# A decoder layer in one kernel: transposed FFN operands stored in parts, x1 loaded a step ahead, the mixer's output sums moved

## Chip, cores and metric

One core of a Trainium2 chip runs the whole kernel. The metric is device time in microseconds, from the first instruction to the last. The kernel before has a median of 1925.28 us over 3 runs (1925.04 to 1928.67).

## What is computed

One decoder layer over 2048 rows of 1024 columns in float32, with a gated-MLP mixer and a SwiGLU feed-forward (2816 hidden), each modulated by six vectors made from `c`:

```python
mod = silu(c) @ mod_w + mod_b
sh1, sc1, g1, sh2, sc2, g2 = split(mod, 6)
h = x * (1 + sc1) + sh1
u, v = split(gelu(h @ w_in + b_in), 2)
v = layer_norm(v, ln_g, ln_b)                    # 1024 columns
sv = w_m @ v per chunk of 128 rows and group of 128 columns + b_s   # w_m: w_s * causal
y = (u * sv) @ w_out
x = layer_norm(ALPHA * x + (1 + g1) * y)         # x1
h = x * (1 + sc2) + sh2                          # h2
g, u = split(h @ ffn_w_in, 2)
y = (silu(g) * u) @ ffn_w_out
out = layer_norm(ALPHA * x + (1 + g2) * y)
```

## The kernel before

**Products in parts.** Every large product runs on TensorE with both operands split into two parts: `parts` (lines 91 to 96) makes hi as a cast on ScalarE (line 94) and lo as a subtraction on VectorE (line 95), both into one tile of 4 KB per partition (UNIT). Three matmuls per product follow, hi by hi, hi by lo, lo by hi. The mixer's output weights `wot` are prepared early and kept in DRAM already in parts; they are loaded straight into the tiles that TensorE reads.

**Rows.** The rows stand in four blocks b of 512, and in two halves sb of two blocks. The mixer (line 274) runs for one half, then for the other: the v product with its layer norm, eight u steps (`u_tile`; a step is two blocks by 24 matmuls) with the spatial products (`s_tile`) from step 3 on, then y.

**y.** y is a Strassen-Winograd product: seven smaller products P1, P2, P6, P5, P7, P3, P4 in that order, each over four k. Their left operands are blocks of u and sums of them: `left_y` (line 388) makes the four sums per k on VectorE (line 393) when P6's operands are made, and then the parts (tiles `y_S`, tag hB). P6, P7 and P4 accumulate in the banks in which P1 lies, after `evacuate` has taken P1's values out (line 409: x times a constant plus the bank, into row r), with x loaded into an xs buffer. Two layer-norm passes follow per half, and x1 goes to DRAM (`x1d`).

**The FFN's left operands.** `h2_part` (line 459) takes one pair of 128-column slices of x1 for one block: TensorE transposes it (line 475), ScalarE modulates (line 476). The FFN is a Strassen-Winograd product too, over blocks A11, A12 (from the even block) and A21, A22 (odd block) with sums S1 to S4. So for the even block A11 and A12 go raw to DRAM (`hop`), and for the odd block they are read back, GpSimd forms the sums (four of them), and A22 and S1 to S4 go raw to `hop`. `tail` (line 782) is the load of x1 (`x1c`, four DMAs) and `h2_part`. The first half's eight tails run in the u steps 0 to 3 of the second half's mixer, two in a step; the second half's run inside the FFN loop. `load_ops` (line 503) reads `hop` and makes the parts, just before the FFN uses them: 28 tiles per half.

**The FFN.** `ffn_in` (line 517) takes 11 column groups, each with seven products for gate and up; the weights' parts are made four products ahead. `ffn_out` (line 669) is the last product.

**What sets the order.** Nearly all DMAs go through SP's one queue in program order, so a DMA that waits holds those behind it. A framework's scheduler fixes each engine's order ahead of time, from the code's order, its own costs and the pools' buffers: lt and xs have 3 row buffers each, late 10, hB 8, w 6, u 16 half rows; in the FFN h3 has 4 rows and hr 2 half rows. A new tile in a buffer waits until the old one's last reader is through, and a DMA store counts as a reader.

Of the kernel before, what the change touches and what calls it, by code (L numbers as in the profile page):

```python
# [37 lines left out]
def gmlp_swiglu_layer(  # L38
# [235 lines left out]
    def mixer(sb, jobs, u_done):  # L274
# [8 lines left out]
        def h_piece(d):  # L283
            if sc1[d] is None:
                mod_of(sh1, 0, d, 0.0, "lt")()
                mod_of(sc1, 1, d, 1.0, ("lc", "bc")[d % 2])()
            for x, b in enumerate(blocks):
                r = new("u", f"xT{b}_{d}", HALF)
                nc.sync.dma_start(out=r, in_=xT[d, :, b * TB : (b + 1) * TB])
                nc.scalar.activation(r, r, AF.Identity, bias=sh1[d], scale=sc1[d])  # L290
                h[x][d] = parts(r, f"h{b}_{d}", ("hA", "hB")[x])
# [211 lines left out]
    def load_ops(sb, names):  # L503
# [277 lines left out]

    def tail(b, i, tag):
# [4 lines left out]
        h2_part(b, i, lambda t, q: x1[:, t, q, :], tag)  # L787

# [99 lines left out]
```

## Time and profile before

| | |
|---|---|
| median of 3 runs | 1925.28 us |
| the profiled execution's own time | 1928.73 us |
| its span in the profile | 1927.0 us |
| TensorE matmuls, weight loads | 1840.4 us (96%), 1519.8 us (79%) |
| VectorE, ScalarE, GpSimd | 1228.4, 688.6, 505.4 us |
| mean granted TensorE clock | 0.979 of full |
| DMA | 359.69 MB, mean 187 GB/s |

TensorE's busy share is an average over stages that differ; the idle time lies in a few places, and after a stop the clock is at its lower level for a while. So the places are read one at a time: the list of waits, then a table of stretches, and in each stretch the chain or the timeline. A matmul of 512 columns shows more than its step in such a list, since successive ones overlap.

### The profile page before, as it was taken

What the parts mean: (1) busy time and instruction counts of PE and PEld (TensorE: products, weight loads), DVE (VectorE), ACT (ScalarE), POOL (GpSimd) and SP (SyncE); (2) the same over time, 40 slices, a digit from 0 to 9 for tenths busy, and PEclk for the clock granted to TensorE, in tenths of its full rate; (3) what the DMA queues carried; (4) which work ended last, traced back from release to release, by engine and by line L of the source; (5) the groups of instructions that cost most, each with busy time, mean ns of one, the idle gap of its engine ahead of it and who ended that gap; (6) DMA issues with size and microseconds to landing.
All of it is one profiled execution on the core that took longest, in us unless ns stands there. A gap on an engine that the chain in (4) does not pass through costs nothing.

```text
span 1927.0 us, 23234 instructions
## 1 busy us (share of the span) xinstructions
PE 1840.4 (96%) x8168; PEld 1519.8 (79%) x8168; DVE 1228.4 (64%) x1785; ACT 688.6 (36%) x1132; POOL 505.4 (26%) x327
## 2 busy tenths in 40 slices
PE   7999989997978799999999999999999999999997
PEld 6888877875867588888887888888888888888886
DVE  7569878241676965545777856767766344446868
ACT  5264152152221443443334533333334233334320
POOL 0000000003000456556543455355533100000104
PEclk9999999998989899999999999999999999999998
DMA  9638875136565634554455535654554666556532
GB/s 379 200 133 318 316 271 197 65 110 207 181 239 193 221 117 170 190 170 149 167 196 179 174 104 192 206 170 159 193 196 170 223 191 187 180 174 185 169 128 98
DMA packets 171015, 359.69 MB, mean 187 GB/s; under 512 B 19953, under 2 KB 36369, under 8 KB 170898
## 3 DMA queue, kind: packets, MB, share of 16 engines
q1 hardware_dynamic: 170834, 358.17, 55.0%
q8 instruction: 64, 1.05, 0.2%
q14 instruction: 53, 0.43, 0.1%
q0 software_dynamic: 64, 0.03, 0.0%
HBM read 251.43 MB, written 106.70 MB: 186 GB/s over the span
## 4 chain that ended last, share of the span: by engine, by line
PE 80%; issue 8%; DVE 5%; DMA 4%; ACT 1%; POOL 1%; SPq 0%; DVEq 0%; POOLq 0%; ACTq 0%
PE o L663 21%; PE v_ps L312 8%; PE u_ps L346 6%; PE y L448 1%; PE f_10g_X L521 1%; PE f_4g_X L521 1%; PE f_2g_X L521 1%; PE f_3g_X L521 1%; PE f_5g_X L521 1%; PE f_1u_X L521 1%; PE f_4u_X L521 1%; PE f_3u_X L521 1%; PE f_2u_X L521 1%; PE f_5u_X L521 1%; PE f_1g_X L521 1%
## 5 line engine op out<-in xcount | busy, mean ns | idle before, releaser
L663 PE MATMUL o<-wd_w,alw 128*128 128x512 f32 x1848 | 419.2, 389 | 0.0
L663 PEld LDWEIGHTS o<-wd_w,alw 128*128 128x128 f32 x1848 | 346.8, 188 | 72.0
L183 POOL TENSOR_TENSOR ln_rss<-ln_ves,mhalf 128x4 f32<-128x4 f32 x7 | 14.4, 2050 | 708.5 <-DVE ln_ves L182 708.5
L312 PE MATMUL v_ps<-wv,h 128*128 128x512 f32 x768 | 178.4, 395 | 16.3 <-ACT h L94 12.5
L346 PE MATMUL u_ps<-h,wu 128*128 128x512 f32 x768 | 185.8, 401 | 2.8 <-ACT wu L94 2.8
L312 PEld LDWEIGHTS v_ps<-wv,h 128*128 128x128 f32 x768 | 146.4, 191 | 47.8 <-ACT h L94 13.0
L448 PE MATMUL y<-y_T,y_S 128*128 128x512 f32 x672 | 161.1, 401 | 18.2 <-ACT y_S L94 12.5
L346 PEld LDWEIGHTS u_ps<-h,wu 128*128 128x128 f32 x768 | 147.0, 193 | 33.9 <-ACT wu L94 3.2
L448 PEld LDWEIGHTS y<-y_T,y_S 128*128 128x128 f32 x672 | 129.8, 194 | 48.7 <-ACT y_S L94 14.5
L95 DVE TENSOR_TENSOR alw<-al,alw 128x512 fp32r<-128x512 f32 x154 | 100.3, 686 | 88.3 <-ACT alw L94 88.3
L94 ACT CAST alw<-al 128x512 fp32r<-128x512 f32 x154 | 89.0, 620 | 142.1 <-PE o L663 139.9
L95 DVE TENSOR_TENSOR wd_w<-wdl,wd_w 128x512 fp32r<-128x512 f32 x77 | 52.9, 689 | 67.1 <-ACT wd_w L94 67.1
L94 ACT CAST wd_w<-wdl 128x512 fp32r<-128x512 f32 x77 | 47.8, 623 | 105.0 <-PE o L663 79.8
L119 DVE SCALAR_TENSOR_TENSOR modw<-modw,cact 128x1024 f32<-128x1024 f32 x48 | 58.4, 1219 | 25.0 <-DMA modw<-in_modwT 25.0
L95 DVE TENSOR_TENSOR wu<-wu_raw,wu 128x512 fp32r<-128x512 f32 x32 | 22.2, 701 | 67.0 <-ACT wu L94 67.0
L351 ACT ACTIVATE u<-u_ps,colc 128x512 f32<-128x512 f32 x32 | 22.0, 689 | 88.1 <-PE u_ps L346 88.1
L94 ACT CAST y_S<-u 128x512 fp32r<-128x512 f32 x48 | 29.2, 620 | 59.3 <-PE y L448 25.7
L95 DVE TENSOR_TENSOR y_S<-u,y_S 128x512 fp32r<-128x512 f32 x48 | 32.4, 685 | 21.5 <-ACT y_S L94 21.5
L94 ACT CAST wv<-wv_raw 128x512 fp32r<-128x512 f32 x32 | 19.8, 620 | 73.2 <-PE v_ps L312 44.9
L183 POOL TENSOR_TENSOR lnv_rss<-lnv_ves,mhalf 128x4 f32<-128x4 f32 x4 | 4.8, 1206 | 156.4 <-ACT wu L94 90.3
L617 DVE TENSOR_TENSOR wd<-wd,g_bc 128x512 f32<-128x512 f32 x44 | 36.5, 855 | 14.0 <-DMA wd<-in_wd 13.6
L95 DVE TENSOR_TENSOR wv<-wv_raw,wv 128x512 fp32r<-128x512 f32 x32 | 21.8, 683 | 25.9 <-ACT wv L94 25.9
(615 smaller groups left out, 3702.9 us busy)
## 6 DMA issues: line engine op xcount, KB each, us to landing
al<-aop SPq DMA_DIRECT2D x154, 256.0 KB, 2.9
modw<-in_modwT SPq DMA_DIRECT2D x48, 512.0 KB, 6.2
aop<-aop_s SPq DMA_DIRECT2D x88, 256.0 KB, 2.0
y_T<-woT SPq DMA_DIRECT2D x32, 512.0 KB, 4.9
y_T<-woB SPq DMA_DIRECT2D x24, 512.0 KB, 6.1
wd<-in_wd SPq DMA_DIRECT2D x44, 256.0 KB, 4.2
wdT<-wd SPq DMA_DIRECT2D x44, 256.0 KB, 4.4
wdl<-wdT SPq DMA_DIRECT2D x44, 256.0 KB, 2.7
```

What stands on the lines that cost most here:

```text
L94: nc.scalar.copy(out=o[:, 0, :], in_=src)
L95: nc.vector.tensor_tensor(out=o[:, 1, :], in0=src, in1=o[:, 0, :].bitcast(F32), op=ALU.subtract)
L119: nc.vector.scalar_tensor_tensor(out=w, in0=w, scalar=1.0, in1=env["cact"], op0=ALU.mult, op1=ALU.mult, accum_out=modc[:, j : j + 1],)
L183: nc.gpsimd.tensor_tensor(out=rs, in0=ve, in1=mhalf.broadcast_to([P, m]), op=ALU.pow)
L312: nc.tensor.matmul(ps[x][t], lhsT=h[x][k][:, part, t * P : (t + 1) * P], rhs=w[:, wpart, :], start=(k == 0 and part == 0 and wpart == 0), ...
L346: nc.tensor.matmul(p, lhsT=w[d // 4][:, wpart, (d % 4) * P : (d % 4 + 1) * P], rhs=h[x][d][:, part, :], start=(d == 0 and wpart == 0 and p ...
L351: nc.scalar.activation(u[x, i], p, AF.Gelu, bias=colc[:, i : i + 1])
L448: nc.tensor.matmul(ps[j], lhsT=a[:, part, j * P : (j + 1) * P], rhs=w[:, wpart, :], start=(k == 0 and part == 0 and wpart == 0 and pr in ( ...
L521: nc.tensor.matmul(ps, lhsT=w[:, wpart, k * P : (k + 1) * P], rhs=a[k][:, part, :], start=(first and k == 0 and wpart == 0 and part == 0), ...
L617: nc.vector.tensor_tensor(out=b, in0=b, in1=env["g2"][:, cs], op=ALU.mult)
L663: nc.tensor.matmul(ps[:, cs], lhsT=a[:, part, p * P : (p + 1) * P], rhs=w[:, wpart, cs], start=(first and part == 0 and wpart == 0), stop= ...
```

## The change

Four things are done.

1. **Parts in DRAM.** `hop` tiles hold parts (512 KB instead of 256). `store` makes the parts where the operand is made, in buffers that alternate between two tags (xs and lt for the first half, h3 and hr for the second), and stores them; `load_ops` loads 28 tiles of parts per half and makes nothing. Since the odd block needs raw A11 and A12, these go raw to new DRAM tiles `hraw` as well. hr is now one full tile.
2. **x1 a step ahead.** `tail_load` is split from `tail`; the first load is issued in the v product, and each step issues the next one's, into a late buffer. There is one tail per u step, 0 to 7, instead of two in each of steps 0 to 3. The columns of g2 (eight modw loads) move from u steps 4 to 7 to steps 6 and 7.
3. **xT of the second half** lies in lt buffers instead of u buffers.
4. **y's sums** are made after the parts of P1 (two of them) and of P2 (the other two).

```diff
-    hop = [[[dram.tile([P, TB], F32, name=f"hop{o}_{k}_{sb}") for sb in range(2)] for k in range(NK)] for o in range(7)]
+    hop = [[[dram.tile([P, 2, TB], F32, name=f"hop{o}_{k}_{sb}") for sb in range(2)] for k in range(NK)] for o in range(7)]
+    hraw = [[[dram.tile([P, TB], F32, name=f"hraw{q}_{k}_{sb}") for sb in range(2)] for k in range(NK)] for q in range(2)]
...
-                r = new("u", f"xT{b}_{d}", HALF)
+                r = new("lt" if sb else "u", f"xT{b}_{d}", HALF)
...
-            if pr == 6:
-                for o, a, b, op in ((t, a21, a22, ALU.add), (a21, a11, a21, ALU.subtract), (a11, t, a11, ALU.subtract), (a12, a12, a11, ALU.subtract)):
-                    nc.vector.tensor_tensor(out=o, in0=a, in1=b, op=op)
-            return parts({1: a11, 2: a12, 6: a11, 5: t, 7: a21, 3: a12, 4: a22}[pr], f"y{sb}_S{pr}{k}", "hB")
+            p = parts({1: a11, 2: a12, 6: a11, 5: t, 7: a21, 3: a12, 4: a22}[pr], f"y{sb}_S{pr}{k}", "hB")
+            sums = {
+                1: ((t, a21, a22, ALU.add), (a21, a11, a21, ALU.subtract)),
+                2: ((a11, t, a11, ALU.subtract), (a12, a12, a11, ALU.subtract)),
+            }
+            for o, a, b, op in sums.get(pr, ()):
+                nc.vector.tensor_tensor(out=o, in0=a, in1=b, op=op)
+            return p
...
         def store(n, src):
-            nc.sync.dma_start(out=hop[A_AT[n]][i][sb], in_=src)
+            ptags.append(ptags.pop(0))
+            o = parts(src, f"h2{n}_{sb}_{i}p", ptags[-1])
+            nc.sync.dma_start(out=hop[A_AT[n]][i][sb], in_=o.bitcast(F32))
...
-            store("A11", h[0])
-            store("A12", h[1])
+            for q, n in enumerate(("A11", "A12")):
+                nc.sync.dma_start(out=hraw[q][i][sb], in_=h[q])
+                store(n, h[q])
...
-                t = new("h3" if sb else "s" if n in ("S3", "A22") else "hr", f"h2{n}r_{sb}_{k}", HALF)
-                nc.sync.dma_start(out=t, in_=hop[A_AT[n]][k][sb])
-                out[n].append(parts(t, f"h2{n}_{sb}_{k}", tag_of(n, k)))
+                t = new(tag_of(n, k), f"h2{n}_{sb}_{k}", UNIT)
+                nc.sync.dma_start(out=t.bitcast(F32), in_=hop[A_AT[n]][k][sb])
+                out[n].append(t)
...
-    for i, f in enumerate(mods(g2, 5, 1.0)):
-        jobs.setdefault(("u", i // 2), []).append(lambda i=i: tail(i // 4, i % 4, "lt"))
-        jobs.setdefault(("u", 4 + i // 2), []).append(f)
+    x1s = {}
+
+    def x1_ahead(i):
+        x1s[i] = tail_load(i // 4, i % 4, "late")
+
+    jobs["v", 1, 6] += (lambda: x1_ahead(0),)
+    for i in range(2 * NK):
+        jobs["u", i] = [lambda i=i: tail(i // 4, i % 4, "lt", ["xs", "lt"], x1s[i])]
+        if i < 2 * NK - 1:
+            jobs["u", i].append(lambda i=i: x1_ahead(i + 1))
+    jobs["u", 6] += mods(g2, 5, 1.0)[:NK]
+    jobs["u", 7] += mods(g2, 5, 1.0)[NK:]
...
-        between[i + 1, 1] = lambda i=i: tail(2, i, "h3")
-        between[i + 2, 6] = lambda i=i: tail(3, i, "h3")
+        between[i + 1, 1] = lambda i=i: tail(2, i, "h3", ["h3", "hr"])
+        between[i + 2, 6] = lambda i=i: tail(3, i, "h3", ["h3", "hr"])
```

The scheduler's order changes at three places that matter below. Names carry the half or block first: `y0_S71` is the left part of product P7, k 1, in y of the first half; `xT2_1` and `h2_1` are slices of block 2.

ScalarE at the end of the first half's y, before:

```order
L94 CAST y0_S70_2338<-u1_0_1280 128x512
L290 ACTIVATE xT2_0_2650<-xT2_0_2650,modc_85 128x512
L94 CAST h2_0_2653<-xT2_0_2650 128x512
L94 CAST y0_S71_2355<-u1_1_1374 128x512
L290 ACTIVATE xT3_0_2656<-xT3_0_2656,modc_85 128x512
L290 ACTIVATE xT2_1_2667<-xT2_1_2667,modc_85 128x512
L94 CAST h2_1_2670<-xT2_1_2667 128x512
L94 CAST y0_S72_2372<-u1_2_1474 128x512
L290 ACTIVATE xT3_1_2673<-xT3_1_2673,modc_85 128x512
```

and with the change:

```order
L94 CAST y0_S70_2354<-u1_0_1296 128x512
L94 CAST y0_S71_2371<-u1_1_1390 128x512
L94 CAST y0_S72_2388<-u1_2_1490 128x512
L94 CAST y0_S73_2405<-u1_3_1590 128x512
L94 CAST y0_S30_2422<-u0_4_1695 128x512
L94 CAST y0_S31_2439<-u0_5_1811 128x512
L94 CAST y0_S32_2456<-u0_6_1905 128x512
```

The activations of xT and the casts behind them are no longer between y's casts.

TensorE in u step 1 of the second half, before (`h2T0_1` are the transposes of tail 1, `u2_1` the u product of block 2):

```order
L346 MATMUL u2_1_ps_3532<-h2_5_2846,wu1_11_3427 128x512 x3
L346 MATMUL u2_1_ps_3532<-h2_6_2887,wu1_11_3427 128x512
L475 MATMUL h2T0_1_ps_3510<-ident_76,x1c0_1_3504 128x128
L475 MATMUL h2T0_5_ps_3516<-ident_76,x1c0_1_3504 128x128
L346 MATMUL u2_1_ps_3532<-h2_6_2887,wu1_11_3427 128x512
L475 MATMUL h2T0_1_ps_3510<-ident_76,x1c0_1_3504 128x128
L475 MATMUL h2T0_5_ps_3516<-ident_76,x1c0_1_3504 128x128
L475 MATMUL h2T0_1_ps_3510<-ident_76,x1c0_1_3504 128x128
L475 MATMUL h2T0_5_ps_3516<-ident_76,x1c0_1_3504 128x128
L346 MATMUL u2_1_ps_3532<-h2_6_2887,wu1_11_3427 128x512
```

and with the change, at the end of that step:

```order
L348 MATMUL u3_1_ps_3568<-h3_6_2909,wu1_11_3448 128x512 x3
L348 MATMUL u3_1_ps_3568<-h3_7_2950,wu1_11_3448 128x512 x3
L483 MATMUL h2T0_1_ps_3596<-ident_76,x1c0_1_3528 128x128 x4
L483 MATMUL h2T0_5_ps_3602<-ident_76,x1c0_1_3528 128x128 x4
L348 MATMUL u2_2_ps_3631<-h2_0_2669,wu1_20_3535 128x512 x2
L348 MATMUL u3_2_ps_3658<-h3_0_2675,wu1_20_3535 128x512 x2
```

Single transposes stood between matmuls, each behind one of the four loads; now the eight of a tail stand together, behind the step's matmuls.

VectorE in y of the second half, before (`r2_0` is row tile 0 of block 2, `y1_1_0` the bank of P1):

```order
L95 TENSOR_TENSOR y1_S23_4446<-u2_7_4201,y1_S23_4446 128x512
L95 TENSOR_TENSOR h2A11_0_0_4287<-h2A11r_0_0_4285,h2A11_0_0_4287 128x512
L95 TENSOR_TENSOR h2A11_0_1_4292<-h2A11r_0_1_4290,h2A11_0_1_4292 128x512
L409 SCALAR_TENSOR_TENSOR r2_0_4327<-x2_00_4430,y1_1_0_4358 128x512
L409 SCALAR_TENSOR_TENSOR r2_1_4328<-x2_10_4433,y1_1_1_4359 128x512
L409 SCALAR_TENSOR_TENSOR r2_2_4329<-x2_20_4436,y1_1_2_4360 128x512
```

and with the change (`h2S1_0_3p` and its like are parts made by the last of the eight tails):

```order
L95 TENSOR_TENSOR h2S1_0_3p_4314<-h2_1_3_4290,h2S1_0_3p_4314 128x512
L95 TENSOR_TENSOR y1_S53_4706<-s1_1_1_4410,y1_S53_4706 128x512
L95 TENSOR_TENSOR h2S2_0_3p_4318<-h2a1_1_3_4303,h2S2_0_3p_4318 128x512
L95 TENSOR_TENSOR h2S4_0_3p_4326<-h2a1_1_3_4303,h2S4_0_3p_4326 128x512
L95 TENSOR_TENSOR h2S3_0_3p_4322<-h2_1_3_4290,h2S3_0_3p_4322 128x512
L415 SCALAR_TENSOR_TENSOR r2_0_4411<-x2_00_4528,y1_1_0_4448 128x512
L83 TENSOR_TENSOR r2_0_4411<-y1_2_0_4540,r2_0_4411 128x512
```

The first evacuation of P1's banks followed P2's left parts; now it follows the last tail's parts.

## Rows read from the trace of the kernel before

**Rows 1.** TensorE's waits over the span: engine, line, awaited: us, times, longest

```profile
PE h2T_ps L475 <- DMA x1c<-x1d: 16.8, 4, 10.6
...
PE y L448 <- ACT y_S L94: 12.5, 4, 8.5
PE f_0g_X L521 <- ACT f_0g_w L94: 8.6, 1, 8.6
...
PE f_10g_X L521 <- ACT f_10g_u L572: 3.7, 1, 3.7
PE y L448 <- ACT xT L290: 3.7, 1, 3.7
...
PE u_ps L346 <- ACT wu L94: 2.8, 1, 2.8
```

**Rows 2.** Stretches: length, busy us (instructions) per engine, granted clock, DMA share, GB/s

```profile
core 0: us, PE busy (x) PEld busy (x) DVE busy (x) ACT busy (x) POOL busy (x), PEclk, DMA share, GB/s
218.00:250.00 32.00, 29.13 (x127) 23.13 (x126) 28.91 (x54) 6.39 (x11) 0.00 (x0) 1.00 0.70 230
250.00:295.00 45.00, 41.30 (x171) 33.68 (x170) 32.52 (x55) 23.17 (x36) 0.00 (x0) 0.92 0.75 271
295.00:330.00 35.00, 31.27 (x132) 25.35 (x131) 32.28 (x58) 9.95 (x16) 3.96 (x2) 0.95 0.55 187
397.00:475.00 78.00, 61.17 (x291) 51.17 (x290) 23.40 (x53) 35.12 (x46) 18.05 (x14) 0.87 0.53 169
530.00:602.00 72.00, 60.34 (x249) 48.47 (x248) 45.57 (x75) 17.50 (x29) 0.00 (x0) 0.91 0.71 248
602.00:668.00 66.00, 49.07 (x192) 37.26 (x191) 60.34 (x88) 20.44 (x36) 18.71 (x10) 0.92 0.50 174
668.00:1050.00 382.00, 382.00 (x1720) 317.08 (x1719) 240.85 (x272) 154.60 (x264) 211.03 (x136) 1.00 0.50 167
1050.00:1075.00 25.00, 21.27 (x83) 17.00 (x82) 18.24 (x25) 14.89 (x27) 6.23 (x4) 0.86 0.74 247
1075.00:1910.00 835.00, 835.00 (x3685) 691.43 (x3684) 525.12 (x713) 294.23 (x501) 229.21 (x141) 1.00 0.52 172
```

**Rows 3.** Groups of TensorE instructions, 397 to 475 us

```profile
L475 PE MATMUL h2T_ps<-ident,x1c 128*128 128x128 f32 x64 | 10.3, 291 | 16.8 <-DMA x1c<-x1d 16.8
L357 PE MATMUL s_ps<-wm,v 128*128 128x128 f32 x32 | 5.8, 357 | 0.0
```

**Rows 4.** Stretch 668 to 1050 us, the transposes of line 475 alone

```profile
668.00:1050.00 382.00, 8.28 (x64) 7.45 (x64) 1.00 0.50 167
```

**Rows 5.** Timeline, 236 to 246 us: start, length, what, [idle before <- releaser]

```profile
241.34 1.22 ACT L94 CAST y_S<-u 128x512 fp32r<-128x512 f32 x2 [10.05 <-DVE u L393]
```

**Rows 6.** The page's DMA issues: count, KB each, median us to landing

```profile
al<-aop SPq DMA_DIRECT2D x154, 256.0 KB, 2.9
modw<-in_modwT SPq DMA_DIRECT2D x48, 512.0 KB, 6.2
```

**Rows 7.** The chain of waits, 455 to 475 us: start, us, what

```profile
457.78 1.60 POOL h2a L86
...
460.81 4.52 DMA hop<-h2a
...
465.40 2.52 DMA x1c<-x1d
```

**Rows 8.** The page's instruction groups: a cast on ScalarE

```profile
L94 ACT CAST y_S<-u 128x512 fp32r<-128x512 f32 x48 | 29.2, 620 | 59.3 <-PE y L448 25.7
```

**Rows 9.** Groups of VectorE instructions, 668 to 1050 us, shapes apart

```profile
L95 DVE TENSOR_TENSOR f_8g_w<-f_8g_b,f_8g_w 128x512 fp32r<-128x512 f32 x7 | 7.4, 1056 | 0.4 <-ACT f_8g_w L94 0.3
```

**Rows 10.** Groups of VectorE instructions, 310 to 390 us, shapes apart

```profile
L95 DVE TENSOR_TENSOR wv<-wv_raw,wv 128x512 fp32r<-128x512 f32 x16 | 10.8, 681 | 20.9 <-ACT wv L94 20.9
```

**Rows 11.** ScalarE's waits over the span

```profile
ACT h2S L94 <- DMA h2S3r<-hop: 30.0, 3, 26.2
```

**Rows 12.** Timeline of VectorE, 604 to 632 us

```profile
621.03 4.86 DVE L429 SCALAR_TENSOR_TENSOR r<-r,ln_rss,ln1b_bc 128x1024 f32<-128x1024 f32 x4
```

More of the change, by code (lines that the diff above doesn't have):

```diff
@@ L457, in mixer, with h2_part @@
         return lambda: norm(1)
-    def h2_part(b, i, cols_of, tag):
+    def h2_part(b, i, cols_of, tag, ptags):
         sb = b // 2
         def store(n, src):
-            nc.sync.dma_start(out=hop[A_AT[n]][i][sb], in_=src)
+            ptags.append(ptags.pop(0))
+            o = parts(src, f"h2{n}_{sb}_{i}p", ptags[-1])
+            nc.sync.dma_start(out=hop[A_AT[n]][i][sb], in_=o.bitcast(F32))
         pair = new(tag, f"h2_{b}_{i}", ROW)
@@ L477, in h2_part @@
         if b % 2 == 0:
-            store("A11", h[0])
-            store("A12", h[1])
+            for q, n in enumerate(("A11", "A12")):
+                nc.sync.dma_start(out=hraw[q][i][sb], in_=h[q])
+                store(n, h[q])
         else:
             pair = new(tag, f"h2a1_{b}_{i}", ROW)
-            for q, n in enumerate(("A11", "A12")):
-                nc.sync.dma_start(out=pair[:, q * 512 : (q + 1) * 512], in_=hop[A_AT[n]][i][sb])
+            for q in range(2):
+                nc.sync.dma_start(out=pair[:, q * 512 : (q + 1) * 512], in_=hraw[q][i][sb])
             a11, a12, a21, a22 = pair[:, lo], pair[:, hi], *h
@@ L780, in mods, with tail_load @@
         return [mod_of(to, k, d, plus) for d in range(ND)]
-    def tail(b, i, tag):
+    def tail_load(b, i, tag):
         x1 = new(tag, f"x1c{b}_{i}", ([P, NT, 2, P], F32))
@@ L786, in tail @@
             nc.sync.dma_start(out=x1[:, t], in_=src[:, t, :, i, :])
-        h2_part(b, i, lambda t, q: x1[:, t, q, :], tag)
+        return x1
+    def tail(b, i, tag, ptags, x1=None):
+        x1 = x1 or tail_load(b, i, tag)
+        h2_part(b, i, lambda t, q: x1[:, t, q, :], tag, ptags)
     def rows_of_ln1():
@@ L802, in gmlp_swiglu_layer @@
         jobs["v", 1, d] = f
-    for i, f in enumerate(mods(g2, 5, 1.0)):
-        jobs.setdefault(("u", i // 2), []).append(lambda i=i: tail(i // 4, i % 4, "lt"))
-        jobs.setdefault(("u", 4 + i // 2), []).append(f)
+    x1s = {}
[8 more added lines that the diff above has]
+    jobs["u", 7] += mods(g2, 5, 1.0)[NK:]
     def following():
         early.close()
-        env["ops"] = phase("right", opsA11=(4, UNIT), opsA12=(4, UNIT), raw2=(4, ROW), hr=(2, HALF))
+        env["ops"] = phase("right", opsA11=(4, UNIT), opsA12=(4, UNIT), raw2=(4, ROW), hr=(1, UNIT))
         ops.update(load_ops(0, ("A11", "A12")))
```

## The prediction

> **What bounds the kernel now.** I began with TensorE's waits [rows 1] and then cut the span into stretches [rows 2]. From 1075 to 1910 us TensorE is busy all the time at granted clock 1.00: 3685 matmuls in 835 us, 0.2266 us each. From 668 to 1050 it has no idle time either (382.00 of 382). What a stretch takes beyond its matmuls times 0.2266 is what can be won there, and it holds both idle time and time at the lower of the two clocks (1.2 against 2.4 GHz):
>
> - 218-250: 32 - 127 x 0.2266 = 3.2
> - 250-295: 45 - 171 x 0.2266 = 6.2
> - 295-330: 35 - 132 x 0.2266 = 5.1
> - 397-475: 64 transposes and 32 spatial products are only 128 columns wide [rows 3]; a transpose takes 8.28/64 = 0.13 us in the loop, where the clock is full [rows 4], and I count both kinds at that. 78 - 195 x 0.2266 - 96 x 0.13 = 21.3
> - 530-602: 72 - 249 x 0.2266 = 15.6
> - 602-668: 66 - 192 x 0.2266 = 22.5
> - 1050-1075: 25 - 83 x 0.2266 = 6.2
>
> Together 80 us of 1927: the most that better feeding of TensorE can give. The rest is arithmetic that the change does not touch.
>
> **The change part by part** (us; minus is a gain).
>
> *y's sums after P1 and P2.* In y of the first half the sums stand last on VectorE before P6, and P6's first cast, with ScalarE idle for 10.05 us, waits for them [rows 5]. Moved up, they are done long before. 218-250: **-3.2**; bounds 0 and -3.2. The same four sums per k cause the 8.5 us wait of y in the second half [rows 1]; there another wait follows, below.
>
> *xT in other buffers.* In y of the first half, ScalarE's order had 16 activations of xT, and the casts of h after them, between the casts that y needs; each waits for an xT load, and that load for a buffer. In the new order the y casts follow one another. The wait through xT (3.7 us in [rows 1]) and its slow clock go: 250-295: **-6.2**; bounds 0 and -6.2. What pays: part of the xT loads and activations now comes after y. The first v weight stands on SP behind three xT loads and an x load. One 256 KB load takes 2.9 us [rows 6], but loads overlap and most are issued before y ends: 295-330: **+1**; bounds 0 and +3.
>
> *x1 one step ahead.* The four waits for x1c (16.8 us in [rows 1]) come from SP's order. The chain shows it: SP held the x1c load until a store of h2a had landed 4.52 us after its issue, then the load took 2.52 [rows 7]. In the new order a tail's transposes stand in one piece at the end of a step, and their load is issued one step (48 x 0.2266 = 10.9 us) before. What can be left is a wait for a weight's cast, of which the u loop has one of 2.8 us [rows 1]. I take half: 21.3 becomes 1.4, **-20**; bounds -21 and -10 (loads of wu behind the doubled stores).
>
> *Second half's y.* Two of eight tails and eight loads of modw slip from the u steps into y. In the new order VectorE takes the first row of P1's result only after every part of the last tail, and P6 accumulates into those same banks: this is the **new wait**. From the tail's transposes to P6, TensorE has 16 short products and P1 and P2: 16 x 0.13 + 96 x 0.2266 = 23.8. The tail's own chain is two evacuations (1.2 at the price of a cast, 0.62 [rows 8]), the first part (a cast and a subtraction of 0.68 [rows 10]: 1.3), four sums of 1.60 on GpSimd [rows 7] and the last part: 1.2 + 1.3 + 6.4 + 1.3 = 10.2. In the same three buffers pass four modw, 6.2 us of load [rows 6] and 1.2 of work each, two at a time 14.8, and a store of 4.5. Sum 29.5, so 6 us late; three more rows behind further x and modw loads, say 3; and the lower clock after such a stop, as now (clock 0.91 over 72 us, 6.5). That is 15, no less than now. Above stands the DMA: the stretch moved 248 GB/s at a share of 0.71, so 349 at full share, 25 MB in 72 us. It had 17.9 MB; the slipped tails' ten stores (5.2), raw reads (1.0), modw (4.2) and the doubled loads of A11 and A12 (2.1) make 30.4, which is 87 us, 15 more than the stretch has now. Below: the sums' wait goes and nothing follows, -10. Not all those bytes must land before y ends, so I stay near the chain: **+4**.
>
> Here a rule speaks against the change. First the rows: a lo part beside GpSimd's sums takes 1.056 us in the loop [rows 9], where GpSimd is busy 211 of 382 us [rows 2], and 0.681 in the v product, where it does little [rows 10]: 0.375 more, 2 us for a tail's five. The Trainium skill, "SBUF — State Buffer", section "Who interferes with whom", says that a VectorE instruction with two SBUF inputs and a GpSimd instruction that reads SBUF shut each other out for the whole instruction. By that, each of the five waits up to a sum, 8 us by estimate, and the time below would be 1896. I go by the rows; their 2 us are inside what I round.
>
> *FFN's start.* The first weight's cast stood behind casts of S3 and S1 on ScalarE, which waited 26.2 us for the hop load [rows 11]. In the new order those 28 casts and subtractions are gone from here (19 us of VectorE's 60.3 in 602-668), and the weight's lo part is left behind the last rows of the layer norm: four of them take 4.86 us [rows 12], one more of that size and three of about half 3.0, 8 in all; then some 3 at the low clock (now 0.08 x 66 = 5). 22.5 becomes 11.5: **-11**; bounds -20 (TensorE starts with the hi part) and -4.
>
> *FFN loop.* 28 parts are added, 17 us on ScalarE (154.6 busy of 382) and at 1.056 30 us on VectorE (240.9). Weights are made four products, 10.9 us, ahead, which covers a cast that waits behind a sum. **+2**; bounds 0 and +10.
>
> *Second half's operands.* ScalarE no longer waits for h2S loads ahead of its copy at 1054 (3.7 us). But 28 loads double to 14.7 MB. Seven sets (of four loads) come free one every 5.4 us (two products of 12 matmuls), the first 33 us before the second half begins, and the last is wanted 33 us after it: 66 us. Beside the loop's 167 GB/s (11 MB) they make 25.7 MB, 74 us at 349 GB/s: 8 late at worst, none if the rest gives way. I take half: 6.2 becomes 4, **-2**; bounds -6 and +4.
>
> Sum: -3.2 - 6.2 + 1 - 20 + 4 - 11 + 2 - 2 = **-35.4**. Against the profiled execution, 1928.73 us (span 1927.0): 1893.3. That execution is 3.45 above the median of three, 1925.28, so I give **1890**.
>
> **The rivals.**
>
> *All is hidden.* The new wait in y does not come, FFN starts on hi parts, doubled loads are in time: -3.2 - 6.2 - 21 - 10 - 16 - 6 = -62: **1863**. For it: DMA share is 0.5 over most of the span. Against it: VectorE's order in y. The Trainium skill, "DMA: Bandwidth & Descriptors", "Anatomy of one DMA", gives 2 us plus the bytes at 436 GB/s, by estimate 3.2 us for 512 KB; by it the four modw take 8.8, the chain 22.2 with a store of 3.2, and no wait comes. The row says 6.2 [rows 6], with other transfers beside it, so I go by that. Chance 0.17.
>
> *DMA bound at both places.* y takes the full +15, the later operands +2 and the loop +6: -35.4 + 11 + 4 + 4 = -16: **1909**. For it: 0.71 and 0.74 shares before the bytes are added. Against: that part can land later. Chance 0.20.
>
> *Slower: buffers that turn over only with their stores.* A part now occupies a buffer until its store lands: 0.62 + 0.68 + 4.5 = 5.8 us. In the loop every second part goes through a single hr buffer; two or three turns in a tail of five parts hold ScalarE up to 17.4 us with the weights' casts queued behind it, 6.5 more than the 10.9 of lead: 26 for four such tails. In y, one at a time, five turns and four modw are 29 + 29.6 against 23.8: 35 late plus clock. In place of +2 and +4 that is +26 and +41 - 15.6 = +25, so -35.4 + 24 + 21 = +10: **1935**. It decides as soon as the two places together lose 35 us more than I count. Against it: the 4.5 is one store in a crowd [rows 7]; a 256 KB load takes 2.9 in the median [rows 6]. Chance 0.08.
>
> *Nothing changes.* x1c, too, waits for a buffer or SP, and the gaps only move: **1925**. Chance 0.04.
>
> **The numbers.** My own case has the remaining 0.51, with 1878 to 1902 as its range. To hold 8 in 10 I reach from most of the first rival to past the second: 1865 to 1914. A difference under 0.2% (3.9 us) is about what a measurement of this kernel cannot tell from none. Faster: my case and the first two rivals, 0.87; same 0.04; slower 0.09.
>
> **What would show it.** Right: no wait for x1c in TensorE's list; no gap before P6 in the first half; a gap before P6 in the second half, released through VectorE's first row r2_0; a first FFN wait of about 8 us for a weight's lo part, with ScalarE not waiting for hop. Wrong: waits for wu or y_T loads in u or y (bandwidth), idle TensorE between 630 and 1015 (hr), or gaps of 8 us and more behind loads of the second half's operands.

## The result, and the profile after

With the change the kernel takes 1896.82 us (median of 4 runs, 1891.33 to 1897.97) against 1925.16 (4 runs, 1925.03 to 1928.67): a ratio of 0.9843, 95% interval 0.982 to 0.9865, or 28 us less. The prediction said 1890, 1865 to 1914. The profiled execution took 1897.97 us (span 1896.3), 30.8 less than that of before; 393.24 MB were moved instead of 359.69, at 207 GB/s instead of 187; the mean granted clock is 0.985.

TensorE's waits over the span, as [rows 1] (engine, line, awaited: us in all, times, longest):

```profile
PE y L454 <- DVE r L415: 12.4, 2, 9.6
PE y L454 <- DMA y_T<-woB: 8.5, 2, 5.1
PE v_ps L314 <- ACT wv L94: 6.8, 2, 6.3
PE f_0u_X L530 <- DVE ln_mvs L180: 6.6, 1, 6.6
PE f_0g_X L530 <- DVE f_0g_w L95: 1.8, 1, 1.8
...
PE u_ps L348 <- ACT wu L94: 1.4, 1, 1.4
...
```

The waits for x1c, for xT, for `y_S` and for the copy of `f_10g_u` are gone. In their place stand a wait for VectorE's row r (9.6 us in one piece), waits for y's weights, a longer wait for the first v weight, and a shorter one at the FFN's start.

The stretches, as [rows 2] (length, busy us and instructions of TensorE, its weight loads, VectorE, ScalarE, GpSimd; granted clock; DMA share; GB/s):

```profile
218.00:250.00 32.00, 32.00 (x143) 26.48 (x142) 28.03 (x46) 8.30 (x14) 0.00 (x0) 1.00 0.70 224
250.00:290.00 40.00, 38.26 (x169) 31.43 (x168) 23.14 (x38) 9.16 (x15) 0.00 (x0) 1.00 0.64 209
290.00:325.00 35.00, 28.72 (x115) 23.17 (x115) 33.39 (x62) 15.87 (x25) 5.68 (x2) 0.90 0.73 257
395.00:480.00 85.00, 84.93 (x440) 72.22 (x439) 42.97 (x76) 41.75 (x62) 13.98 (x10) 1.00 0.61 206
498.00:606.00 108.00, 85.78 (x347) 68.68 (x345) 72.02 (x124) 18.35 (x30) 7.99 (x5) 0.89 0.84 294
606.00:650.00 44.00, 33.88 (x133) 26.25 (x132) 40.47 (x52) 14.35 (x24) 16.80 (x11) 0.88 0.91 339
650.00:1010.00 360.00, 360.00 (x1622) 298.65 (x1621) 256.55 (x277) 154.74 (x267) 207.40 (x130) 1.00 0.55 193
1010.00:1045.00 35.00, 35.00 (x156) 28.99 (x155) 18.08 (x21) 11.72 (x20) 14.38 (x10) 1.00 0.94 367
```

By the prediction's own count (0.2266 us for each matmul of 512 columns), 218-250 loses nothing, where it lost 3.2; 250-290 loses 1.7 (6.2 before); 290-325 8.9 (5.1); the u steps nothing (21.3), with TensorE busy for 84.93 of 85 us at clock 1.00; the loop nothing, as before; and 1010 to 1045, where 6.2 were lost, nothing, though the DMA share there is 0.94 at 367 GB/s. The second half's y, now at 498 to 606, loses 29.4 and the FFN's start 13.9. These two cannot be set beside the 15.6 and 22.5 of before one by one, since 530 to 602 held only 249 of y's 336 matmuls and the next stretch the rest. A comparison needs the same matmuls on both sides. TensorE's timeline shows where this y begins and where its last group of 96 ends, before:

```profile
529.30 22.02 PE L448 MATMUL y<-y_T,y_S 128*128 128x512 f32 x96
...
599.81 22.04 PE L448 MATMUL y<-y_T,y_S 128*128 128x512 f32 x96 [1.92 <-DMA y_T<-woT]
```

and after:

```profile
498.95 13.86 PE L454 MATMUL y<-y_T,y_S 128*128 128x512 f32 x60
...
582.69 23.59 PE L454 MATMUL y<-y_T,y_S 128*128 128x512 f32 x96 [5.10 <-DMA y_T<-woB]
```

So this y took 92.5 us and now takes 107.3. Measured like this through the whole span (the table below the experiments), the stages that became shorter give 50 us, at the x1 loads, in y of the first half, at the FFN's start and at the second half's operands, and 19 us were given back, 15 of them in one place, y of the second half. The trace shows how. ScalarE around 515 us:

```profile
514.31 0.62 ACT L94 CAST y_S<-u 128x512 fp32r<-128x512 f32 x1 [2.71 <-DVE u L399]
518.28 1.45 ACT L484 ACTIVATE h<-h2T_ps,modc 128x512 f32<-128x512 f32 x2 [3.35 <-DVE modw L119]
```

The last tail's transposes were done at 495.6, as the u steps ended. ScalarE writes their modulated pair only at 518.28, released by VectorE's work on `modw`: the pair needs an lt buffer, and a modw of g2 holds it. VectorE, in order, takes P1's first row behind the tail's last part:

```profile
528.61 0.69 DVE L95 TENSOR_TENSOR h2S_3p<-h,h2S_3p 128x512 fp32r<-128x512 f32 x1
...
535.11 2.04 DVE L95 TENSOR_TENSOR h2S_3p<-h2a,h2S_3p 128x512 fp32r<-128x512 f32 x2 [4.97 <-ACT h2S_3p L94]
537.06 0.69 DVE L95 TENSOR_TENSOR h2S_3p<-h,h2S_3p 128x512 fp32r<-128x512 f32 x1
537.67 0.68 DVE L415 SCALAR_TENSOR_TENSOR r<-x,y 128x512 f32<-128x512 f32 x1
```

TensorE went on at 538.4. Between the pair and the last parts lies one more wait. The tail reads A11 and A12 back from DRAM for the sums; SP, in order, issued these loads only at 525.78, and GpSimd had stood 8.4 us when they were there:

```profile
531.83 1.26 POOL L86 TENSOR_TENSOR h<-h2a,h 128x512 f32<-128x512 f32 x1 [8.36 <-DMA h2a<-hraw]
```

In the same stretch the queue is full:

```profile
480.00:520.00 40.00, 35.31 (x186) 29.78 (x185) 36.49 (x54) 16.20 (x27) 6.25 (x4) 0.97 1.02 398
```

At 398 GB/s a 512 KB transfer lands each 1.3 us, and those issued there land 8 to 11 us later. The two waits for y_T (3.4 us from 513, 5.1 from 578) are of that kind: these loads landed 9.8 and 13.7 us after their issue.

### The profile page after: what moved, and what is told of

It is laid out like the page before. It is cut to its first block, busy times and chain, and to the rows that moved or that the text cites. A ratio compares the mean times of both kernels' runs of the same rounds, so it can differ in the third digit from the quotient of the medians.

```text
span 1896.3 us, 23225 instructions
## 1 busy us (share of the span) xinstructions
PE 1829.6 (96%) x8168; PEld 1513.0 (80%) x8168; DVE 1251.6 (66%) x1785; ACT 687.5 (36%) x1132; POOL 513.7 (27%) x327
## 2 busy tenths in 40 slices
DMA packets 173319, 393.24 MB, mean 207 GB/s; under 512 B 20209, under 2 KB 36625, under 8 KB 173202
## 4 chain that ended last, share of the span: by engine, by line
PE 86%; DVE 4%; issue 4%; DMA 3%; ACT 1%; POOL 0%; SPq 0%; DVEq 0%; ACTq 0%; POOLq 0%
PE o L672 21%; PE u_ps L348 8%; PE v_ps L314 8%; PE y L454 4%; PE s_ps L359 1%; PE f_4g_X L530 1%; PE f_3g_X L530 1%; PE f_5g_X L530 1%; PE f_2g_X L530 1%; PE f_2u_X L530 1%; PE f_1u_X L530 1%; PE f_4u_X L530 1%; PE f_3u_X L530 1%; PE f_5u_X L530 1%; PE f_6g_X L530 1%
## 5 line engine op out<-in xcount | busy, mean ns | idle before, releaser
L454 PE MATMUL y<-y_T,y_S 128*128 128x512 f32 x672 | 161.8, 403 | 24.0 <-DVE r L415 12.4
L348 PE MATMUL u_ps<-h,wu 128*128 128x512 f32 x768 | 180.4, 394 | 1.4 <-ACT wu L94 1.4
L119 DVE SCALAR_TENSOR_TENSOR modw<-modw,cact 128x1024 f32<-128x1024 f32 x48 | 58.4, 1220 | 14.1 <-DMA modw<-in_modwT 13.9
L495 POOL TENSOR_TENSOR h<-h 128x512 f32<-128x512 f32 x8 | 11.9, 1486 | 146.3 <-DMA x1c<-x1d 54.0
L95 DVE TENSOR_TENSOR wu<-wu_raw,wu 128x512 fp32r<-128x512 f32 x32 | 21.3, 688 | 43.8 <-ACT wu L94 43.8
L94 ACT CAST wu<-wu_raw 128x512 fp32r<-128x512 f32 x32 | 18.7, 619 | 57.1 <-PE v_ps L314 36.3
```

Of the source, the lines that this page charges most:

```text
L94: nc.scalar.copy(out=o[:, 0, :], in_=src)
L95: nc.vector.tensor_tensor(out=o[:, 1, :], in0=src, in1=o[:, 0, :].bitcast(F32), op=ALU.subtract)
L119: nc.vector.scalar_tensor_tensor(out=w, in0=w, scalar=1.0, in1=env["cact"], op0=ALU.mult, op1=ALU.mult, accum_out=modc[:, j : j + 1],)
L348: nc.tensor.matmul(p, lhsT=w[d // 4][:, wpart, (d % 4) * P : (d % 4 + 1) * P], rhs=h[x][d][:, part, :], start=(d == 0 and wpart == 0 and p ...
L454: nc.tensor.matmul(ps[j], lhsT=a[:, part, j * P : (j + 1) * P], rhs=w[:, wpart, :], start=(k == 0 and part == 0 and wpart == 0 and pr in ( ...
L495: nc.gpsimd.tensor_tensor(out=a22, in0=a21, in1=a22, op=ALU.add)
```

## The experiments

Each kernel differs from the changed one (or from the experiment that is named) by the lines shown; ... marks lines left out, which belong to the same edit. All ratios are to the kernel before, measured beside it on the same chip. The runs come from several chips, on which the kernel before took 1923.65 to 1926.96 us, so a difference of 3 us between two medians says little unless the ratios bear it out. Where a stage's length is given, it is of the profiled execution, from the stage's first matmul to its last. Undoing one part of the change gave:

| part undone | median us | ratio, 95% interval | against the change |
|---|---|---|---|
| none | 1896.82 | 0.9843 (0.982 to 0.9865) | |
| parts in DRAM (e6) | 1898.93 | 0.9862 (0.9848 to 0.9877) | 2 slower, the intervals overlap |
| x1 a step ahead (e7) | 1915.27 | 0.9943 (0.9928 to 0.9958) | 18 slower |
| xT in lt (e4) | 1895.04 | 0.9847 (0.9826 to 0.9868) | no difference |
| sums after P1 and P2 (e3) | 1908.37 | 0.9915 (0.9888 to 0.9942) | 12 slower |

**e7: no x1 ahead.** Each tail loads x1 in its own step, and into an lt buffer instead of a late one.

```diff
-    jobs["v", 1, 6] += (lambda: x1_ahead(0),)
-        jobs["u", i] = [lambda i=i: tail(i // 4, i % 4, "lt", ["xs", "lt"], x1s[i])]
-            jobs["u", i].append(lambda i=i: x1_ahead(i + 1))
+        jobs["u", i] = [lambda i=i: tail(i // 4, i % 4, "lt", ["xs", "lt"])]
```

> Each tail loads x1 in its own u step into an lt buffer, one tail a step; the other three parts of the change stay. Theory A (the load a step ahead is what took the waits for x1c away): waits for x1c of 2 to 5 us in most of the eight steps come back, 1912 to 1930. Theory B (one tail a step in place of two is enough): TensorE waits for x1c under 4 us in all, 1895 to 1901.

1915.27 us. TensorE's waits:

```profile
PE h2T_ps L483 <- DMA x1c<-x1d: 30.4, 3, 23.5
...
PE y L454 <- DMA y_T<-woT: 6.3, 2, 3.7
```

Theory A, but with another spread than I wrote: not some us in most steps, but three waits, 23.5 of the 30.4 us in the last. There SP issued the load at 527.38, behind four modw loads for the same lt buffers. So e7 takes away two things, the early load and its own buffer, and does not tell them apart. The u steps take 146.0 us instead of 108.7. In y, then, the wait for row r is 0.9 in all instead of 12.4, and y takes 87.6 instead of 107.3: of the 37 us lost, about 20 come back there, and 18 are seen in the time.

**e3: the sums at P6 again.**

```diff
-            sums = {
-                1: ((t, a21, a22, ALU.add), (a21, a11, a21, ALU.subtract)),
-                2: ((a11, t, a11, ALU.subtract), (a12, a12, a11, ALU.subtract)),
-            }
-            for o, a, b, op in sums.get(pr, ()):
-                nc.vector.tensor_tensor(out=o, in0=a, in1=b, op=op)
...
+            if pr == 6:
+                for o, a, b, op in ((t, a21, a22, ALU.add), (a21, a11, a21, ALU.subtract), (a11, t, a11, ALU.subtract), (a12, a12, a11, ALU.subtract)):
+                    nc.vector.tensor_tensor(out=o, in0=a, in1=b, op=op)
```

> y's sums are made at P6 again, the rest as in the change. Theory A (the sums were what P6 of the first half waited for; in the second half they are hidden behind the new wait for r2_0): a gap of 2 to 4 us comes back before P6 of the first half and little is added in the second: 1899 to 1903. Theory B (the sums matter as much in the second half): also 5 us or more before P6 there: 1904 to 1910.

1908.37 us, 11.5 more. In the first half y is no longer than in the change (78.6 us and 78.4; it was 86.8 before); 0.8 us came back before P6:

```profile
216.70 24.07 PE L450 MATMUL y<-y_T,y_S 128*128 128x512 f32 x104
241.57 31.14 PE L450 MATMUL y<-y_T,y_S 128*128 128x512 f32 x136 [0.80 <-DVE y_S L95]
...
```

In the second half:

```profile
PE y L450 <- ACT y_S L94: 30.9, 1, 30.9
```

One wait of 30.9 us, where the change has waits of 9.6 and 2.8 for row r and 8.5 for y_T; y takes 116.1 us instead of 107.3. The sums then stand behind the row that waits for the tail, and P6 gets its left operand last. So theory B: the sums' move pays in the second half, and in the first, with xT out of y, next to nothing hangs on it.

**e4: xT in the u buffers again.**

```diff
-                r = new("lt" if sb else "u", f"xT{b}_{d}", HALF)
+                r = new("u", f"xT{b}_{d}", HALF)
```

> xT of the second half lies in the u buffers again, the rest as in the change. Theory A (what xT's move saves in y of the first half, it pays at the start of v, where TensorE now waits 6.3 us for a weight against 3.7 before): the 3.7 us wait for xT comes back in y, the wait at v's start falls to 3 to 4: 1894 to 1901, no difference from the change. Theory B (my prediction's sum): 5 us slower than the change, 1900 to 1905.

1895.04 us: theory A in the time. The wait at the start of v falls back from 6.3 to 3.7 us. The wait of 3.7 us in y does not come back; there is one of 1.3 for a cast of h, made from xT, and y of the first half takes 78.0 us, no more than in the change:

```profile
218.99 54.70 PE L454 MATMUL y<-y_T,y_S 128*128 128x512 f32 x240
274.95 22.03 PE L454 MATMUL y<-y_T,y_S 128*128 128x512 f32 x96 [1.26 <-ACT h L94]
```

Time is lost before it: this y begins at 219.0 and not at 215.6, and the u loop ahead of it has the wait of 2.8 us for wu again that it had before the change (1.4 with the change).

**e6: hop raw, parts when loaded.**

```diff
-            ptags.append(ptags.pop(0))
-            o = parts(src, f"h2{n}_{sb}_{i}p", ptags[-1])
-            nc.sync.dma_start(out=hop[A_AT[n]][i][sb], in_=o.bitcast(F32))
+            nc.sync.dma_start(out=hop[A_AT[n]][i][sb], in_=src)
...
-                t = new(tag_of(n, k), f"h2{n}_{sb}_{k}", UNIT)
-                nc.sync.dma_start(out=t.bitcast(F32), in_=hop[A_AT[n]][k][sb])
-                out[n].append(t)
+                t = new("h3" if sb else "s" if n in ("S3", "A22") else "hr", f"h2{n}r_{sb}_{k}", HALF)
+                nc.sync.dma_start(out=t, in_=hop[A_AT[n]][k][sb])
+                out[n].append(parts(t, f"h2{n}_{sb}_{k}", tag_of(n, k)))
...
```

> Parts of the FFN's left operands are made when they are loaded again, hop holds raw values, hr has two half rows; the other three parts of the change stay. Theory A (parts in DRAM pay at the FFN's start, 8 us, and at the second half's operands, 6, and cost in y through the doubled traffic and the longer tails): y of the second half loses 10 us less, the FFN's start 8 to 12 more and 1040 to 1075 about 6 more: 1897 to 1906. Theory B (my prediction's sum: 13 us gained there, 4 lost in y): 1906 to 1912.

1898.93 us: theory A. The largest part of the change, and all of its traffic, gives 2 us, which the intervals do not tell from nothing. What it gains is there:

```profile
PE f_0g_X L527 <- ACT f_0g_w L94: 5.3, 1, 5.3
...
PE f_10g_X L527 <- ACT f_10g_u L578: 4.4, 1, 4.4
PE f_0g_X L527 <- DVE h2S L95: 3.8, 2, 3.4
...
```

These return without it; y, in exchange, has no wait for row r and takes 89.1 us instead of 107.3. So parts in DRAM cost 18 us in y and give 15 at the FFN's start and 7 at the second half's operands.

**e1: the g2 columns in the v product.**

```diff
-    jobs["u", 6] += mods(g2, 5, 1.0)[:NK]
-    jobs["u", 7] += mods(g2, 5, 1.0)[NK:]
+    for d, f in enumerate(mods(g2, 5, 1.0)):
+        jobs["v", 1, d] += (f,)
```

> The eight g2 columns (modw40 to 47) are loaded and multiplied in the second half's v product instead of after u steps 6 and 7. Theory A (modw40 and 41 hold the lt buffers that the last tail's modulated pair needs, ScalarE's activation starts at 518 only behind modw41's read, and everything up to r2_0 follows): the wait of P6 for r2_0 (9.6 and 2.8 us) goes, the y_T waits (8.5 us) shrink by the about 5 us that four modw take of the DMA queue, time 1877 to 1884. Theory B (the last tail's own chain of sums and parts is too long, whatever stands in the buffers): the wait stays at 7 us or more, time 1892 to 1898.

1882.22 us (0.9784, 0.9758 to 0.9811), 14.6 less than the change: the time is theory A's. y of the second half takes 91.1 us, not 107.3. The waits are theory A's only in part:

```profile
PE y L454 <- DVE r L415: 8.5, 2, 8.1
...
PE y L454 <- DMA y_T<-woT: 0.3, 1, 0.3
```

The waits for y_T are gone (0.3 us of 8.5), and ScalarE writes the last pair at 498.6 and not 518.3. But 8.1 us before P6 stay, with another releaser:

```profile
521.76 0.69 DVE L95 TENSOR_TENSOR h2S_3p<-h,h2S_3p 128x512 fp32r<-128x512 f32 x1 [0.68 <-ACT h2S_3p L94]
...
527.85 0.69 DVE L415 SCALAR_TENSOR_TENSOR r<-x,y 128x512 f32<-128x512 f32 x1 [4.19 <-DMA x<-in_x]
```

VectorE now has the tail behind it at 522.5 and stands 4.2 us for x, whose load was issued at 518.47, behind a store of the tail's parts, into a queue 9 us long. So theory A's cause was one of two in a row. The eight loads that moved are also 4.2 MB less in a full queue; e1 does not tell that from the buffers.

**e2: the g2 columns at u steps 4 to 7,** as before the change.

```diff
-    jobs["u", 6] += mods(g2, 5, 1.0)[:NK]
-    jobs["u", 7] += mods(g2, 5, 1.0)[NK:]
+    for i, f in enumerate(mods(g2, 5, 1.0)):
+        jobs["u", 4 + i // 2].append(f)
```

> The g2 columns stand at u steps 4 to 7, one pair a step, as before the change; the rest as in the change. Theory A: two pairs leave y, so P6's wait falls to 0 to 5 us, but each pair shares the lt buffers with a tail, so waits of 1 to 3 us a step can come in the u steps: 1885 to 1897. Theory B: the wait of P6 stays near 9 us and nothing changes in u: 1894 to 1900.

1908.71 us (0.9919), 12 slower than the change, outside both: a miss. The waits in y are all there (10.2 for row r, 6.8 and 1.7 for y_T, 4.1 for the pair), and the FFN's start has 17.3 instead of 10.1. Four modw loads are still issued in y, at 515 to 538. Most of the 12 us are lost at the FFN's start: from y's end through its first 168 matmuls it takes 61.0 us and not 51.7. There VectorE takes a row from y's banks only at 623.12, when its x has landed at 623.02, and the first weight's lo part stands behind that row, at 624.45.

**e5: e1, and A11 and A12 loaded after y.**

```diff
-        ops.update(load_ops(0, ("A11", "A12")))
-    ops.update(load_ops(0, ("S1", "S2")))
+    ops.update(load_ops(0, ("A11", "A12", "S1", "S2")))
```

> As e1 (g2 columns in the v product, 1882), and the eight loads of A11 and A12 (4 MB) stand after y in the program instead of ahead of it. With the g2 columns gone, P6 still waited 8.1 us, for x2_00, whose load was issued at 518.5 and landed at 527.8, in a DMA queue that moves 512 KB each 1.25 us. Theory A (the queue: eight loads are 10 us of it): the wait falls to 0 to 3 us, time 1873 to 1879. Theory B (x2_00 is held by SP's order behind the store of S1's parts, which waits for the last tail's sums): the wait stays at 6 us or more, 1880 to 1886.

1882.31 us, and the same 8.1 us, but this is no evidence for B. The scheduler, which knows no reason to wait, put the eight loads back ahead of y; on SP only one y_T load changed its place. It shows how near two runs of nearly one kernel come (1882.22 and 1882.31).

**e8: e1, and x for P1 in the hr buffer.**

```diff
...
+            if sb and (x, cs.start) == (0, 0):
+                if t % 2 == 0:
+                    xq[0] = new("hr", f"xq{t}", ROW)
+                xt = xq[0][:, (lo, hi)[t % 2]]
+            else:
                 xt = new("xs", f"x{blocks[x]}_{t}{cs.start}", HALF)
```

> As e1 (1882), and the x tiles for P1 of the second half lie in the hr buffer, which nothing else uses in y, two at a time, instead of xs buffers that the last tail's parts occupy. Theory A (x2_00's place in the queue is what P6 waits for): the wait falls from 8.1 to 0 to 3 us, 1873 to 1879. Theory B (VectorE's order and the tail's sums, done at 518, are as late): 4 us or more stay, 1879 to 1883.

1878.73 us (0.9757, 0.9742 to 0.9771): theory A in the wait and in the time. x is issued at 506.6 and has landed at 515; the waits for row r fall from 8.5 to 2.8:

```profile
PE y L461 <- DMA y_T<-woT: 3.5, 3, 1.9
PE y L461 <- DVE r L422: 2.8, 1, 2.8
```

But y did not become shorter: 91.1 us in e1 and in e8. The waits for y_T are 3.5 where e1 had 0.3, and from 498 to 590 the mean granted clock is 0.94 and not 0.96, so that TensorE is busy 82.7 us with the same 337 matmuls instead of 79.7. Of the 3.5 us that the time fell, 2 lie at the FFN's start; so it is not shown that the shorter wait for row r paid.

**e10: e1 with hop raw** (the lines of e6).

> As e1 (1882), with raw hop as in e6. e6 was within 2 us of the change: parts in DRAM gained 13 us at the FFN's start and at the second half's operands, and lost as much in y. Theory A (the loss in y came from modw in the tails' buffers and the full queue, so with the g2 columns gone parts in DRAM pay): 1888 to 1893. Theory B (parts in DRAM give nothing in any setting): 1880 to 1885.

1891.98 us (0.9825, 0.9803 to 0.9847; the four runs lie between 1887.53 and 1896.34), 10 more than e1 by the medians and 8 by the ratios: theory A. Without the eight loads of g2 in y, parts in DRAM are worth 8 to 10 us; in the change as it stands, 2. They still cost time in y: it takes 80.5 us in e10 and 91.1 in e1, a difference of 11 where e6 had 18.

**e11: e8 with xT in the u buffers** (the line of e4).

> As e8 (1879), with xT of the second half in the u buffers as before the change. Theory A (as in e4, the wait in y and the wait at v's start trade against each other): 1876 to 1881. Theory B (without the xT tiles in lt, the modw loads in v find free buffers earlier and the start of v is 3 us shorter at no cost): 1873 to 1876.

1890.63 us (0.9817), 12 more: a miss for both. The start of v is 3.2 us shorter, but y of the first half now waits:

```profile
PE y L461 <- DVE r L83: 8.5, 1, 8.5
...
PE v_ps L314 <- ACT wv L94: 3.5, 1, 3.5
```

VectorE stood there 5.8 us for a part of h and then 2.4 for a load of x. y of the first half takes 91.6 us, against 77.3 in e8. So with the modw loads where e1 puts them, xT's place does matter.

**e9: e8, two row tiles of the layer norm on ScalarE and GpSimd.**

```diff
+                if sb and x == 0 and t > 1:
+                    nc.scalar.activation(r, r, AF.Identity, bias=nm, scale=rs)
+                    nc.gpsimd.tensor_tensor(out=r, in0=r, in1=env["ln1g"], op=ALU.mult)
+                    nc.gpsimd.tensor_tensor(out=r, in0=r, in1=env["ln1b"], op=ALU.add)
...
```

> As e8 (1879), and two of the four row tiles of block 2 get their layer norm's scaling from ScalarE and GpSimd instead of VectorE, whose four instructions of 1.28 us after y's end stand ahead of the first FFN weight's lo part. Theory A (that work is what the FFN's start waits for): two of four instructions go, and two of the earlier four; the waits at the FFN's start, now 8.5 us in all, fall by 2.5 to 4, time 1874 to 1877. Theory B (GpSimd's reads hold VectorE back, or the next wait takes over): 1878 to 1882.

1884.44 us (0.9796), 6 slower than e8 and outside both ranges: B's reason, and more of it than B said. The waits at the FFN's start are 16.4 us in all, against 9.1 in e8. In the timeline, VectorE:

```profile
588.70 8.45 DVE L446 SCALAR_TENSOR_TENSOR r<-r,ln_mvs,ln1g_bc 128x1024 f32<-128x1024 f32 x3
...
598.39 0.68 DVE L95 TENSOR_TENSOR f_0g_w<-f_0g_b,f_0g_w 128x512 fp32r<-128x512 f32 x1
```

and GpSimd:

```profile
583.92 5.59 POOL L443 TENSOR_TENSOR r<-r,ln1g_bc 128x1024 f32<-128x1024 f32 x2 [2.35 <-ACT r L442]
589.47 6.60 POOL L444 TENSOR_TENSOR r<-r,ln1b_bc 128x1024 f32<-128x1024 f32 x2
```

Three instructions that take 1.2 us each with GpSimd idle (four in 4.87 after the change, below) take 8.45 here, while GpSimd's four run, 2.8 to 3.3 us each.

**e12: e8, and the first two v weights of the second half in the sv buffers.**

```diff
-            r = new("xs", f"wv{sb}_{y}{k}_raw", HALF)
+            r = new("sv" if sb and y == 0 and k < 2 else "xs", f"wv{sb}_{y}{k}_raw", HALF)
```

> As e8 (1879), and the first two v weights of the second half are loaded into the two sv buffers, which nothing uses between the u steps of the two halves, instead of xs buffers. At the start of v TensorE waits 6.7 us there for a cast that stands on ScalarE behind parts of xT and on SP behind xT loads. Theory A (order alone: the weight is needed first, xT slice 3 only 16 us later): the wait and its slow clock go, time 1869 to 1873. Theory B (the xT slices are as late, and the wait comes back within v as a wait for h): 1875 to 1880.

1868.9 us (5 runs, 1867.23 to 1873.37), ratio 0.9711 (0.9688 to 0.9735): theory A, and the best version, 28 us under the change (25 by the ratios). No wait for a v weight is left:

```profile
PE f_0u_X L537 <- ACT f_0u_w L94: 5.1, 1, 5.1
PE y L461 <- DMA y_T<-woT: 4.9, 4, 1.9
...
PE v_ps L314 <- DVE v L83: 0.5, 1, 0.5
```

Against e8, y's end to the first u matmul is 7.7 us shorter. Another 4 us come from y of the second half, and the reason for these is not shown.

## Why the prediction was right, and where it was not

Lengths of the stages, each from one matmul to another that is the same in both traces (us; profiled executions):

| stage | before | after | difference | predicted |
|---|---|---|---|---|
| up to y of the first half | 218.0 | 215.6 | -2.4 | 0 |
| y, first half | 86.8 | 78.4 | -8.3 | -9.4 (-3.2 sums, -6.2 xT) |
| y's end to the first u matmul | 92.5 | 96.2 | +3.6 | +1 |
| u steps with the tails (x1 ahead) | 132.0 | 108.7 | -23.3 | -20 |
| y, second half | 92.5 | 107.3 | +14.8 | +4 |
| y's end through the FFN's first 168 matmuls (a column group) | 60.7 | 51.7 | -9.0 | -11 |
| the FFN's loop in the first half | 367.1 | 367.6 | +0.5 | +2 |
| 280 matmuls around the change of halves | 70.2 | 63.5 | -6.7 | -2 |
| together | | | -30.8 | -35.4 |

The total is 4.6 us from the forecast, but one term alone is 10.8 off; the others, -3.3 and -4.7 above all, make up for more than half of it. That part of the closeness is luck.

- *x1 one step ahead.* Right in cause: no wait for x1c is left, and e7, without the load ahead and without its buffer, has 30.4 us of them. The gain is 3 us more than forecast and beyond the bound of -21. Some of that is the price of the short products: the u steps, now without a gap, take 108.7 us, which leaves 0.113 us for each of their 192 products of 128 columns, not 0.13.
- *Second half's y.* The mechanism was right (VectorE's first row behind the last tail, P6 behind that row); the term was mis-sized, +14.8 for +4. I let modw pass two at a time beside the tail. In the trace the tail's pair stood behind them from 498 to 518. The tail's own chain then took not 10.2 us but 19.4 to the first row: my sum counts the reading back of A11 and A12 as bytes and not as a step of the chain, and GpSimd stood 8.4 us for it. I also took the DMA's limit as a thing that might not bite, and y waited 8.5 us for weights, which I had named as a sign of being wrong. The 349 GB/s that I worked out was no limit: the queue moved 398 here, and the profile before already had 379 in its first 48 us. The upper end that I named, +15, was nearly it. e1 takes 16 us back in this stage and so shows the cause, the g2 loads; how much of it is buffers and how much the queue was not tried.
- *y in the first half: sums and xT.* I added two gains, -3.2 for the sums and -6.2 for xT. The sum is nearly right (-8.3), but not because two gains add: with xT moved and the sums at P6 (e3) this y takes 78.6 us, with the sums moved and xT in the u buffers (e4) 78.0, with both 78.4. Either alone is enough.
- *xT at the start of v.* The bound of +3 was too low (+3.6). The weight's load stood on SP behind six xT loads, to 295.88, and its cast came at 299.67; e12 shows it, by moving the weight to a buffer of its own. Against this stand 2.4 us that I had not forecast, ahead of y: in the eleven traces with xT in lt the first half's y begins between 214.5 and 216.9 us, in the three with xT in u (before, e4, e11) between 218.0 and 219.0. By e4 cost and gain cancel.
- *The sums' move* pays its 9 to 12 us in the second half (e3), where I let the new wait swallow it.
- *FFN's start.* The 28 casts and subtractions are gone, and the four rows stand in front as forecast:

```profile
608.17 4.87 DVE L435 SCALAR_TENSOR_TENSOR r<-r,ln_rss,ln1b_bc 128x1024 f32<-128x1024 f32 x4
612.95 0.68 DVE L415 SCALAR_TENSOR_TENSOR r<-x,y 128x512 f32<-128x512 f32 x1
...
614.26 1.23 DVE L434 SCALAR_TENSOR_TENSOR r<-r,ln_mvs,ln1g_bc 128x1024 f32<-128x1024 f32 x1
...
616.12 0.64 DVE L95 TENSOR_TENSOR f_0g_w<-f_0g_b,f_0g_w 128x512 fp32r<-128x512 f32 x1
```

  The lo part ends 10.5 us after y, not 8. But TensorE's longest wait there, 6.6 us, is not for it. It is for the hi part of the second weight, which my sum left out:

```profile
613.67 0.62 ACT L94 CAST f_0u_w<-f_0u_b 128x512 fp32r<-128x512 f32 x1 [6.74 <-DMA h2S<-hop]
```

  The view puts ScalarE's wait down to a hop load, but the cast's own wait is for VectorE, whose row of 612.95 ended just before. So hop loads did not hold ScalarE, and the same four rows held two weights, not one. For lo parts TensorE waited 1.8 and 1.0 us.
- *Second half's operands.* I held half of a DMA limit against it. 0.94 of the queue's time at 367 GB/s was enough, so all of it came: the 280 matmuls take 63.5 us, which is 280 x 0.2266.
- *The rule on shared reads.* The prediction went by a row that gave 0.375 us more per part. By the Trainium skill, "SBUF — State Buffer", section "Who interferes with whom", the two engines shut each other out, and a part would wait up to a whole sum, 1.6 us by estimate. The parts of S in the loop:

```profile
L95 DVE TENSOR_TENSOR h2S_0p<-h2a,h2S_0p 128x512 fp32r<-128x512 f32 x2 | 3.3, 1668 | 0.1
...
L95 DVE TENSOR_TENSOR h2S_0p<-h,h2S_0p 128x512 fp32r<-128x512 f32 x2 | 3.2, 1576 | 0.3 <-ACT h2S_0p L94 0.3
```

  1.58 to 1.67 against 0.68 alone, 0.9 to 1.0 more: about midway between the two. The parts of A in the same view, at 1.03 to 1.40, are nearer the row. In e9 three instructions took 1.6 us more each than alone, which the rule allows. It cost nothing in the loop, which has room. That the measured time, 1896.8, is the 1896 of this rival is chance: in y the last tail's four parts of S took 0.69 to 1.21 us, and the time was lost elsewhere.
- *The rivals.* "Slower" did not come: the loop shows no wait, though its parts pass through the one hr buffer. "All is hidden" (1863) did not come either. One reason for it was the estimate of 3.2 us for 512 KB from the Trainium skill, "DMA: Bandwidth & Descriptors", "Anatomy of one DMA", a fit for transfers that GpSimd issues. In y's queue a modw, issued by SP, took 9.9 us in the median (480 to 520 us). e12 comes near that time (1868.9), with three more moves. "DMA bound at both places" was right about y's weights and wrong about the later operands and the loop.

## What to carry to other kernels

When work is moved to an earlier stage, look first at the buffers and the queue that it will share there and at what else wants them: the change's largest part was worth 2 us beside eight loads in the same buffers and 8 to 10 without them. Three moves to stages and buffers that had room (e1, e8, e12) then lowered the time by about as much again as the change had.

A part that shows no gain when it is undone alone may still be able to give one: in y of the first half either of two moves takes the whole 8 us, so undoing one shows nothing. And a shorter wait is not yet a shorter stage: in e8 the wait for row r fell by 5.7 us, and y stayed at 91.1. So compare stages from the same matmul to the same matmul, not only the list of waits.

## What the runs showed of the hardware that was not expected

- The DMA queue moved 398 GB/s over 40 us, mostly in 512 KB transfers, where the prediction had worked out 349 as the most from one stretch. A transfer issued there landed 8 to 11 us later.
- Beside GpSimd's instructions, VectorE's went at GpSimd's pace (2.8 us each instead of 1.2 in e9), so work handed to GpSimd slowed what it was to relieve.
